# The first eight attention score rows of a hybrid encoder layer, asked for in another order

## The chip, the cores and the metric

The kernel runs on one core of one Trainium2 chip. The metric is the device time of one execution in microseconds (us). Three runs of the kernel before took 1035.21, 1035.52 and 1036.41 us; the median is 1035.52.

## What is computed

One encoder layer over 1024 tokens of width 1024, in float32. One normed input is multiplied by one projection matrix. Its columns feed two token mixers: group A, windowed attention with 8 query heads over 2 key/value heads, partial rotary turning of the first 16 of 64 dimensions and a sink logit per head; and group B, neighbourhood attention of 8 heads over a 16 x 64 grid. Both results are normed, joined and multiplied by an output matrix, and a gated MLP with a short convolution and a last norm follow. The change lies in group A:

```python
def block(args):
    ...
    s = jnp.einsum('bqgrd,bkgd->bgrqk', q_i, k_i).astype(jnp.float32) * scale
    ...
    m = jnp.maximum(jnp.max(s, axis=-1), sink_gr)
    p = jnp.exp(s - m[..., None])
    denom = jnp.sum(p, axis=-1) + jnp.exp(sink_gr - m)
    o = jnp.einsum('bgrqk,bkgd->bgrqd', p.astype(v_i.dtype), v_i)
    o = o / denom[..., None].astype(o.dtype)
```

## The kernel before, in words

All matrices stand transposed on the chip, features on the 128 partitions and tokens along the row. The projection is made in 18 jobs (`Project`, line 624), each for 128 output columns in two halves of 512 tokens. A half is eight k steps, and a k step is three matmuls (lines 172 to 174), since each operand is kept as a high and a low part. The weights of a job come by DMA (line 150), are split on ScalarE (line 156) and VectorE or GpSimd (line 157), and the product leaves PSUM through line 269 or 273 on VectorE.

Attention is cut into units. A unit of group A is one block of 128 queries of one key/value head: four score rows, one for each of its query heads 0 to 3, and then the products with the values. A score row (`q_step`, line 509) is

- two matmuls on TensorE (line 434) into one of two PSUM banks named s: 128 queries by 256 keys in block 0, which has one neighbour, by 384 in block 1;
- on VectorE mask, sum and minimum out of that bank (line 464), which frees the bank;
- the exponential with its row sum on ScalarE (line 468), the reciprocal on VectorE (line 469);
- then by `PATH_A = "DPTT"`: head 0 splits on ScalarE and VectorE (lines 483, 485) and head 1 on ScalarE and GpSimd (lines 472, 478, 479), and both are transposed by a DMA on SyncE's queue (line 490); heads 2 and 3 are scaled on GpSimd (line 472) and later transposed on TensorE (line 496), and copied out by ScalarE and VectorE (lines 499, 500).

The value products (line 523) read the transposed rows, heads 0 and 1 first, heads 2 and 3 after.

Heads 0 and 1 of the first key/value head come from projection job 1, heads 2 and 3 from job 2. After its projection a job's tile is turned by position (`rotate`, lines 285 to 291, through DMAs and VectorE) and split into two parts that are laid over each other on the partitions. For job 1 the split writes into place (`split_first`, line 305). For job 2 (`split_pair`, line 294) the second part is made by line 299 on VectorE, and DMAs (lines 300 and 302) carry the pieces to their partitions. Job 3, the key and value of the second key/value head, comes next: lines 357 to 362 and 375 measure and split its value, lines 287 to 289 turn its key, and line 341 splits that.

TensorE's order is written out by hand (`manual_schedule`): the list `queue_q` holds all score rows by unit and head, and `fill(n)` puts n k steps of the projection between them. The other engines and the DMA queues are ordered by the scheduler from the program and its priorities, so the order written for TensorE changes theirs too. Each of them works off its order from the front.

The first eight score rows, those of units 0 and 1, are asked for ahead of the unit loop (lines 960 to 964): two at once, then four k steps, then each further row behind two k steps, and two k steps at the end. Then the unit loop begins with the transposes and value products of unit 0.

## Time and profile before

| | |
|---|---|
| profiled execution | 1035.44 us |
| span of its instructions | 1033.6 us |
| TensorE (PE) busy | 1011.4 us, 98% |
| VectorE (DVE) busy | 880.5 us, 85% |
| ScalarE (ACT) busy | 677.1 us, 66% |
| GpSimd (POOL) busy | 215.1 us, 21% |
| mean granted TensorE clock | 0.996 |

Times inside the profile count from the first instruction. Matmuls are pipelined: one of 512 columns is shown as 0.39 us long, though the next one starts 0.23 us after it, so the pace of TensorE is read from the starts. A bracket such as `[3.04 <-DVE hl L485]` is the idle time just before an instruction and what the profile takes for its releaser; where several things are waited for, the one named is that whose signal came last by the profile, and it can be another.

### The profile page before, as it was taken

Reading aid. Unit: us, or ns where it says so; the run is one execution under the profiler, and the core shown is the slowest. Engines: PE = TensorE matmul, PEld = TensorE weight load, DVE = VectorE, ACT = ScalarE, POOL = GpSimd, SP = SyncE. Lnnn points to the kernel's source line nnn. Section 1 sums busy time; section 2 is a strip of 40 time slices with the busy share of each in tenths; the row PEclk is TensorE's granted clock in tenths of the full one; section 3 lists DMA queues with packets and bytes.
Section 4 is the critical chain, followed back from the end, with each engine's and each line's share of the span. In section 5 each row is a group of like instructions: output and inputs, shape, how many; then the busy total and the mean of one; then the engine's idle time right before and its main releaser. Section 6 shows DMA issues by size and latency. Waiting matters only on the chain.

```text
span 1033.6 us, 15700 instructions
## 1 busy us (share of the span) xinstructions
PE 1011.4 (98%) x5102; PEld 578.2 (56%) x5102; DVE 880.5 (85%) x1746; ACT 677.1 (66%) x1242; POOL 215.1 (21%) x340
## 2 busy tenths in 40 slices
PE   8989999999999999999999999999999999999996
PEld 6877777777775545544444444444444444444446
DVE  6798988766898699899898988888888879999864
ACT  7557787777687587645778777754535656555551
POOL 1325555676866301000000000000000000000002
PEclk9999999999999999999999999999999999999999
DMA  8566574777689775300687867733232779878734
GB/s 306 201 138 129 106 131 100 149 164 140 139 179 221 233 260 199 112 1 28 219 271 265 278 232 248 252 110 135 83 112 102 247 251 307 306 244 269 260 133 163
DMA packets 143939, 191.80 MB, mean 186 GB/s; under 512 B 77360, under 2 KB 88112, under 8 KB 143856
## 3 DMA queue, kind: packets, MB, share of 16 engines
q1 hardware_dynamic: 133264, 164.84, 55.4%
q10 hardware_dynamic: 10592, 25.95, 6.6%
q8 instruction: 40, 0.66, 0.3%
q14 instruction: 43, 0.35, 0.1%
HBM read 132.81 MB, written 28.57 MB: 156 GB/s over the span
## 4 chain that ended last, share of the span: by engine, by line
PE 73%; DVE 5%; DMA 1%; ACT 1%; issue 1%; POOL 0%; DVEq 0%; ACTq 0%; POOLq 0%
PE dn L1186 6%; PE dn L1185 6%; PE dn L1184 6%; PE pj L180 6%; PE z L1186 5%; PE z L1184 5%; PE z L1185 5%; PE y L1186 4%; PE y L1184 4%; PE y L1185 4%; PE x L1184 4%; PE x L1186 4%; PE x L1185 4%; PE pj L172 2%; PE pj L174 2%; PE pj L173 2%
## 5 line engine op out<-in xcount | busy, mean ns | idle before, releaser
L1186 PEld LDWEIGHTS <-wlo 128*128 128x128 f16 x898 | 87.9, 98 | 101.3
L1184 PEld LDWEIGHTS <-whi 128*128 128x128 f16 x898 | 88.1, 98 | 100.2
L1185 PEld LDWEIGHTS <-whi 128*128 128x128 f16 x898 | 87.9, 98 | 100.3
L1185 PE MATMUL dn<-xd,whi 128*128 128x512 f16 (+1 forms) x330 | 120.4, 365 | 0.0
L1186 PE MATMUL dn<-xd,wlo 128*128 128x512 f16 (+1 forms) x330 | 120.4, 365 | 0.0
L1184 PE MATMUL dn<-xd,whi 128*128 128x512 f16 (+1 forms) x330 | 120.4, 365 | 0.0
L172 PE MATMUL pj<-xgh,whi 128*128 128x512 f32 x248 | 107.3, 433 | 0.0
L468 ACT ACTIVATE p<-p,nm 128x385 f32<-128x385 f32 (+3 forms) x128 | 74.8, 585 | 38.9 <-DVE nm L464 32.1
L1184 PE MATMUL z<-hg,whi 128*128 128x512 f16 x264 | 100.1, 379 | 0.0
L1185 PE MATMUL z<-hg,whi 128*128 128x512 f16 x264 | 100.1, 379 | 0.0
L1186 PE MATMUL z<-hg,wlo 128*128 128x512 f16 x264 | 100.1, 379 | 0.0
L174 PE MATMUL pj<-xgh,wlo 128*128 128x512 f32 x248 | 98.5, 397 | 0.0
L173 PE MATMUL pj<-xgl,whi 128*128 128x512 f32 x248 | 97.9, 395 | 0.0
L1158 ACT ACTIVATE whi<-ws,m 128x512 f16<-128x512 f32 (+1 forms) x96 | 65.8, 708 | 37.1 <-DVE ws L1325 22.6
L1159 DVE SCALAR_TENSOR_TENSOR wlo<-ws,m,whi 128x512 f16<-128x512 f32 (+1 forms) x96 | 70.1, 740 | 16.5 <-ACT whi L1158 16.3
L1039 POOL TENSOR_TENSOR back<-back,cst 128x4 f32<-128x4 f32 (+1 forms) x7 | 2.8, 394 | 356.8 <-DVE back L1038 356.8
L1173 ACT ACTIVATE scan<-scan 128x1024 f32<-128x1024 f32 (+1 forms) x60 | 61.0, 1017 | 16.6 <-DMA scan<-in_w_down_dram 13.7
L1158 ACT ACTIVATE whi<-raw,m 128x512 f16<-128x512 f32 (+1 forms) x78 | 51.4, 699 | 15.7 <-DMA raw<-in_w_down_dram 9.0
L1159 DVE SCALAR_TENSOR_TENSOR wlo<-raw,m,whi 128x512 f16<-128x512 f32 (+1 forms) x78 | 55.4, 731 | 6.4 <-ACT whi L1158 6.2
L1184 PE MATMUL y<-hg,whi 128*128 128x512 f16 x160 | 60.6, 379 | 0.0
L1185 PE MATMUL y<-hg,whi 128*128 128x512 f16 x160 | 60.6, 379 | 0.0
L1186 PE MATMUL y<-hg,wlo 128*128 128x512 f16 x160 | 60.6, 379 | 0.0
(298 smaller groups left out, 2463.8 us busy)
## 6 DMA issues: line engine op xcount, KB each, us to landing
xd<-x SPq DMA_DIRECT2D x77, 256.0 KB, 5.4
raw<-in_w_down_dram SPq DMA_DIRECT2D x64, 256.0 KB, 3.5
x<-c ACTq DMA_DIRECT2D x22, 512.0 KB, 2.8
scan<-in_w_gate_dram SPq DMA_DIRECT2D x18, 512.0 KB, 4.0
scan<-in_w_up_dram SPq DMA_DIRECT2D x18, 512.0 KB, 4.2
raw<-in_w_gate_dram SPq DMA_DIRECT2D x18, 512.0 KB, 4.4
raw<-in_w_up_dram SPq DMA_DIRECT2D x18, 512.0 KB, 3.6
raw<-in_w_in_dram SPq DMA_DIRECT2D x32, 256.0 KB, 3.1
```

Source lines behind the costliest of these rows:

```text
L172: nc.tensor.matmul(ps, w[0], x[0][:, tsl(h)], start=first, stop=False)
L173: nc.tensor.matmul(ps, w[0], x[1][:, tsl(h)], start=False, stop=False)
L174: nc.tensor.matmul(ps, w[1], x[0][:, tsl(h)], start=False, stop=last)
L180: nc.tensor.matmul(ps, a, b, start=i == 0 and b is x[h][0] and a is w[0], stop=i == len(ws) - 1 and a is w[1])
L468: nc.scalar.activation(p[:, 0:e], p[:, 0:e], AF.Exp, bias=nm, scale=-1.0, accum_out=sm)
L1039: nc.gpsimd.tensor_tensor(back, back, unit_back.to_broadcast([128, n]), op=ALU.mult)
L1158: mark["whi"] = nc.scalar.activation(hi, src, AF.Copy, scale=by)
L1159: nc.vector.scalar_tensor_tensor(lo, src, by, hi, op0=ALU.mult, op1=ALU.subtract)
L1173: nc.scalar.activation(t, t, AF.Square, accum_out=dst)
L1184: nc.tensor.matmul(ps, w[0], x[0], start=first and i == 0, stop=False, skip_group_check=True)
L1185: nc.tensor.matmul(ps, w[0], x[1], start=False, stop=False, skip_group_check=True)
L1186: nc.tensor.matmul(ps, w[1], x[0], start=False, stop=last and i == len(ws) - 1, skip_group_check=True)
```

## The change

The first eight entries of `queue_q` are put into another order: heads 0 and 1 of unit 0, heads 0 and 1 of unit 1, heads 2 and 3 of unit 0, heads 2 and 3 of unit 1. The k steps between them become two before every row from the third on, and four after the eighth, in place of four, then two each, and two after. Rows, k steps and their sum are the same.

```diff
         queue_q = [(u, s) for u in range(len(flat)) for s in flat[u][0]]
+        queue_q[0:8] = [queue_q[4 * u + j] for j0 in (0, 2) for u in range(2) for j in (j0, j0 + 1)]
...
             if i > 1:
-                fill(4 if i == 2 else 2)
+                fill(2)
             run_q([item])
-        fill(FILL1 - 10)
+        fill(FILL1 - 8)
```

On TensorE, before, this stands behind the first two score rows and their four k steps; `q_572` and `q_573` are heads 2 and 3, `q_540` and `q_541` heads 0 and 1, and the number behind `s` or `pj` is that of the buffer:

```order
L174 MATMUL pj_646<-xgh_124,wlo_500 128x512
L434 MATMUL s_654<-ka_534,q_572 128x256
L434 MATMUL s_654<-kb_535,q_572 128x256
L172 MATMUL pj_646<-xgh_201,whi_499 128x512
L173 MATMUL pj_646<-xgl_202,whi_499 128x512
L174 MATMUL pj_646<-xgh_201,wlo_500 128x512
L172 MATMUL pj_646<-xgh_217,whi_499 128x512
L173 MATMUL pj_646<-xgl_218,whi_499 128x512
L174 MATMUL pj_646<-xgh_217,wlo_500 128x512
L434 MATMUL s_671<-ka_534,q_573 128x256
L434 MATMUL s_671<-kb_535,q_573 128x256
```

And this stands in the changed kernel from the third and fourth score row, heads 0 and 1 of unit 1, to the fifth, the first that reads `q_572`:

```order
L434 MATMUL s_669<-ka_534,q_541 128x384
L434 MATMUL s_669<-kb_535,q_541 128x384
L172 MATMUL pj_662<-xgh_201,whi_499 128x512
L173 MATMUL pj_662<-xgl_202,whi_499 128x512
L174 MATMUL pj_662<-xgh_201,wlo_500 128x512
L172 MATMUL pj_662<-xgh_217,whi_499 128x512
L173 MATMUL pj_662<-xgl_218,whi_499 128x512
L174 MATMUL pj_662<-xgh_217,wlo_500 128x512
L434 MATMUL s_690<-ka_534,q_572 128x256
L434 MATMUL s_690<-kb_535,q_572 128x256
```

The first row that needs head 2 moved from the third place to the fifth; before the change four k steps lie ahead of it, and now four k steps and two other score rows. From the first transpose of unit 0 on, TensorE's order is the same.

VectorE, before, behind the second score row's line 464 and the first reciprocal:

```order
L157 TENSOR_TENSOR wlo_584<-raw_579,whi_583 128x512
L482 TENSOR_SCALAR by_620<-sm_613 128x1
L469 RECIPROCAL sm_630<-sm_630 128x1
L287 TENSOR_TENSOR f_172<-f_172,turns_170 64x128 x2
L357 TENSOR_REDUCE top_716<-t_503 64x1
L485 SCALAR_TENSOR_TENSOR hl_619<-p_611,by_620,hl_619 128x2x128
```

And in the changed kernel at the same place, `s_646` and `s_669` being the third and fourth score row:

```order
L464 ISA p_649,nm_650<-s_646,cst_89,nsink_168 128x384
L464 ISA nm_650 128x1
L482 TENSOR_SCALAR by_620<-sm_613 128x1
L469 RECIPROCAL sm_630<-sm_630 128x1
L157 TENSOR_TENSOR wlo_584<-raw_579,whi_583 128x512
L464 ISA p_672,nm_673<-s_669,cst_89,nsink_168 128x384
L464 ISA nm_673 128x1
L485 SCALAR_TENSOR_TENSOR hl_619<-p_611,by_620,hl_619 128x2x128
```

Two more score rows are worked off here, ahead of job 3's turning and measuring (lines 287 and 357). Those and what follows from them (lines 288, 289, 358 to 362, 375, 341) come later.

VectorE, before, where the transposed rows of unit 0's head 3 are written (`pt_863`), which the third value product of unit 0 reads:

```order
L269 TENSOR_TENSOR t_767<-pj_768,rstd1_370 128x512
L469 RECIPROCAL sm_839<-sm_839 128x1
L500 TENSOR_TENSOR turned_653<-pt_863,turned_653 128x2x128
L482 TENSOR_SCALAR by_844<-sm_839 128x1
L464 ISA p_871,nm_872<-s_868,cst_89,nsink_168 128x384
```

And in the changed kernel:

```order
L469 RECIPROCAL sm_839<-sm_839 128x1
L500 TENSOR_TENSOR turned_689<-pt_863,turned_689 128x2x128
L482 TENSOR_SCALAR by_844<-sm_839 128x1
L464 ISA p_871,nm_872<-s_868,cst_89,nsink_168 128x384
L464 ISA nm_872 128x1
L287 TENSOR_TENSOR f_172<-f_172,turns_170 128x128
```

One of the two line 287 instructions of job 4's turning, and its lines 288 and 289 further on, now stand behind this `L500`; before the change they stand ahead of it. On VectorE the two orders agree again from about the 380th of its 1,748 instructions on, on SyncE's queue from about the 95th of 564.

## The prediction

> **What bounds the kernel now.** I read the page's first lines first, then the busy time by stages, then TensorE's waits, then the rows around the longest of them. The page:

> ```profile
> span 1033.6 us, 15700 instructions
> PE 1011.4 (98%) x5102; PEld 578.2 (56%) x5102; DVE 880.5 (85%) x1746; ACT 677.1 (66%) x1242; POOL 215.1 (21%) x340
> ```

> TensorE is busy 98% of the span, so the end moves only by what TensorE waits or runs slowly. The profiled execution took 1035.44 us, 1.84 more than its span and 0.08 under the median of 1035.52; sums below are made against 1035.44. A measurement of this kernel can tell about 0.2%, 2.07 us, from no change. By stages (columns: stretch, length, busy time with counts of PE, PEld, DVE, ACT, POOL, granted clock, DMA share, GB/s):

> ```profile
> 62.20:65.20 3.00, 0.04 (x1) 0.00 (x0) 2.94 (x9) 1.53 (x4) 1.48 (x3) 1.00 0.89 225
> 65.20:70.00 4.80, 4.72 (x16) 3.91 (x17) 3.92 (x15) 2.38 (x5) 1.36 (x6) 0.64 0.36 77
> 77.00:100.00 23.00, 21.79 (x126) 16.30 (x124) 20.41 (x67) 16.77 (x44) 11.99 (x24) 1.00 0.71 136
> 200.00:225.00 25.00, 25.00 (x137) 19.54 (x137) 15.51 (x58) 15.24 (x37) 17.70 (x26) 1.00 0.85 171
> 430.00:800.00 370.00, 370.00 (x1726) 169.05 (x1724) 328.25 (x487) 235.57 (x372) 7.95 (x23) 1.00 0.48 164
> ```

> TensorE stands still for 3 us from 62.2, and then runs 4.8 us at a mean clock of 0.64. VectorE is nearly full there and until 100. Later, as from 200 on, TensorE is full and VectorE has 9.5 us free in 25: what is gained or lost ahead of that is carried to the end. TensorE's waits of the whole run (total, times, longest), and the rows of its timeline at them:

> ```profile
> PE pt L496 <- POOL p L472: 3.8, 4, 1.2
> PE s L434 <- DVE hl L485: 3.0, 1, 3.0
> ...
> 59.21 0.28 PE L434 MATMUL s<-kb,q 128*128 128x256 f32 x1
> 59.33 0.40 PE L172 MATMUL pj<-xgh,whi 128*128 128x512 f32 x1
> ...
> 65.28 0.36 PE L434 MATMUL s<-ka,q 128*128 128x256 f32 x1 [3.04 <-DVE hl L485]
> 77.10 0.38 PE L496 MATMUL pt<-cst,p 128*128 128x128 f32 x2
> 81.30 0.41 PE L523 MATMUL o<-turned,v 128*128 128x256 f16 x2
> 87.83 0.55 PE L496 MATMUL pt<-cst,p 128*128 128x128 f32 x3 [1.21 <-POOL p L472]
> ```

> The longest wait is that of the third score row, head 2 of unit 0, at 65.28. The page puts it down to line 485, which writes nothing that this row reads. It reads the query tile of heads 2 and 3, and that comes by DMA; the tile's rows, and the DMAs' in SyncE's queue:

> ```profile
> L302 SPq DMA_DIRECT2D q<-t x1: 547/547/547, 61.4 to 61.4; - x1
> DMA to landing us min/median/max: 3.8/3.8/3.8
> ...
> 60.76 1.16 SPq L302 DMA_DIRECT2D q<-t x2
> ```

> The second of the two is issued at 61.4 and lands 3.8 later, at 65.2: that is the releaser.

> **The change part by part.** *The wait and the clock.* The 3.04 us go. The slow stretch behind them loses 4.80 x (1 - 0.64) = 1.73 more. No other row of stillness is followed by one: the stretch 77 to 100 holds the wait of 1.21 and has a clock of 1.00. So 1.73 is put down to the long wait, and 4.77 us are to be had.

> [...]

> *What is late next on TensorE.* The third row is now head 0 of unit 1 with 384 keys; its query tile is there, but it needs the first score bank, which line 464 of the first row frees:

> ```profile
> 59.51 1.21 DVE L299 SCALAR_TENSOR_TENSOR t<-t,q 128x1024 fp32r<-128x1024 f32 x1
> 60.65 0.48 DVE L464 CUSTOM_DVE_ANT_0 p<-s,cst,nsink 128x256 f32<-128x256 f32 x1
> ```

> The pace of TensorE's projection matmuls and of a 384 wide score's two, by their starts:

> ```profile
> 60.03 0.40 PE L172 MATMUL pj<-xgh,whi 128*128 128x512 f32 x1
> 60.26 0.39 PE L173 MATMUL pj<-xgl,whi 128*128 128x512 f32 x1
> 70.17 0.33 PE L434 MATMUL s<-ka,q 128*128 128x384 f32 x1
> 70.34 0.34 PE L434 MATMUL s<-kb,q 128*128 128x384 f32 x1
> ```

> Line 464 ends at 61.13. TensorE is there after two k steps: 59.33 + 6 x 0.23 = 60.71. It waits 0.45 and starts at about 61.2. Two score rows of 2 x 0.17 = 0.34 and two pairs of k steps of 6 x 0.23 = 1.38 bring it to 64.6, where head 2 of unit 0 needs the DMA of 65.2. The SyncE and VectorE orders up to that DMA are unchanged, so it lands as before: 0.6 more.

> So 1.05 of waits replace 4.77: TensorE reaches the first transpose, line 496, 3.72 earlier, at 73.4 instead of 77.1. The scores themselves and the k steps cost what they did.

> *VectorE behind it.* It must keep up, and this is where I expect part of the gain to go back. TensorE's third value product of unit 0 (81.30) reads the rows that line 500 writes at 80.98; TensorE comes there at 81.30 - 3.72 = 77.6. VectorE's stretch from the first line 464 to the end of that line 500, with the rows that now stand behind it and the two idle times of note:

> ```profile
> 60.65:81.38 20.73, 17.69 (x81) 14.13 (x80) 18.77 (x59) 11.92 (x29) 7.33 (x18) 0.92 0.71 150
> ...
> 67.98 1.28 DVE L375 SCALAR_TENSOR_TENSOR vhl<-t,down,vhl 64x1024 f16<-64x1024 f32 x1 [0.69 <-ACT vhl L374]
> 72.11 0.69 DVE L269 TENSOR_TENSOR t<-pj,rstd 128x512 f32<-128x512 f32 x1 [0.69 <-PE pj L174]
> 77.19 0.64 DVE L287 TENSOR_TENSOR f<-f,turns 128x128 f32<-128x128 f32 x2
> 77.87 0.43 DVE L288 TENSOR_TENSOR f<-f,turns 128x256 f32<-128x256 f32 x1
> 78.34 0.61 DVE L289 TENSOR_TENSOR f<-f 128x256 f32<-128x256 f32 x1
> 80.98 0.40 DVE L500 TENSOR_TENSOR turned<-pt,turned 128x256 f16<-128x256 f32 x1
> ```

> 18.77 of 20.73 are busy, 1.96 idle. Half of line 287 (0.32), line 288 (0.43) and line 289 (0.61) move behind: 1.36 less work, 17.41. With no idle time line 500 would end at 60.65 + 17.41 = 78.06, with all of it at 80.02. The wait for TensorE (0.69) goes, since TensorE is ahead by then; the wait for ScalarE in front of line 375 stays, since its scale still comes just before it; of the other 0.58 I keep half. That gives 78.06 + 0.69 + 0.29 = 79.04, against 81.38: TensorE waits 1.4 at this product and is 2.34 ahead. The bounds are 81.38 - 80.02 = 1.36 and TensorE's own 3.72 - 0.41, 3.3.

> *The wait at 87.83.* Its chain runs through ScalarE and GpSimd:

> ```profile
> 83.67 1.05 ACT L297 ACTIVATE q<-t 128x1024 fp32r<-128x1024 f32 x1
> 84.62 0.51 ACT L478 ACTIVATE stage<-p 128x384 f16<-128x384 f32 x1
> ...
> 85.21 1.76 POOL L479 TENSOR_TENSOR stage<-p,stage 128x384 f16<-128x384 f32 x1 [1.15 <-ACT stage L478]
> 87.19 1.57 POOL L472 TENSOR_SCALAR p<-p,sm 128x384 f32<-128x384 f32 x2
> ```

> Line 478 stood behind job 4's line 297; now line 297 comes after it, up to 1.05 less. The wait of 1.21 can shrink by as much, or not at all, if the reciprocal (line 469) on VectorE is then the last; I take 0.45, a little under the middle. Sum: 2.34 + 0.45 = 2.8.

> *What is moved past.* SyncE's transposes of unit 1 now stand ahead of job 3's DMAs and of one weight load (line 150). That load and its split on ScalarE, before:

> ```profile
> 70.64 1.00 SPq L150 DMA_DIRECT2D raw<-in_w_in_dram  x1
> ...
> 86.75 0.63 ACT L156 ACTIVATE whi<-raw 128x512 fp32r<-128x512 f32 x1
> ```

> 16 us lie between them and cover it; past that TensorE would wait for each further microsecond. Job 3's pieces are for the second key/value head, whose first unit is the ninth; the seven units between cover them. Both cost nothing.

> The other engines' orders stay shuffled for some way after 88; with 2.6 us idle on VectorE in 77 to 100 and 9.5 from 200 to 225, I give this no mean effect and 1 us to either side. Forecast: 1035.44 - 2.8 = 1032.64, say 1032.7.

> **The rivals.** *VectorE sets the pace.* It is busy 89% from 77 to 100; if none of its idle time closes up, only the moved 1.36 is gained: 1035.44 - 1.36 = 1034.1, no difference that can be told. For it: each idle time has a chain behind it. Against: 0.69 of it waits for the very TensorE that comes earlier. 0.22.

> *The change doesn't reach the wait.* If the third row had waited for VectorE's line 485, as the page names it, the fifth would wait in its place: 1035.4. The landing at 65.2 speaks against it. 0.04.

> *The clock drop is not the wait's.* Then the new order keeps it, and 3.72 - 1.73 = 1.99 remain: 1033.45, just inside what can't be told. Against: it begins right behind the wait, and the median of three runs is within 0.08 of this one. 0.06. [...]

> *Slower: the waits fall into half clock.* If VectorE closes up nothing, TensorE waits 80.02 - 77.6 = 2.4 at the third value product, not far from the 3.04 that dropped the clock; another 1.73 then makes 1.36 - 1.73 = -0.37, 1035.8. If the same happens again at the transpose of 87.83, another 1.73: 1037.5. It decides from a second drop on. Against it: 1.21 of stillness left the clock at 1.00. One drop 0.03, two 0.05.

> **How the numbers follow.** Forecast (2.1 to 4 us gained) 0.60; the rivals 0.22, 0.04, 0.06, 0.03 and 0.05. Faster by over 0.2%: 0.60. Within: 0.22 + 0.04 + 0.06 + 0.03 = 0.35. Slower: 0.05. The range: its low end is all of 3.72 with 0.45 at 87.83, 1031.3; its high end takes in the paced case and the unreached wait, 1035.4. Outside lie the slower cases and what gains more than 4.2.

> **What would show it.** Right: the third score row starts at about 61.2 with 0.45 idle before it, the fifth at 65.3 with 0.6, no clock below 1.00 from 60 to 80, the first line 496 at 73.4, the third value product waiting about 1.4 for line 500, the line 496 of before's 87.83 at about 85. Wrong: a wait of over 2 us left at 65, a second stretch under full clock, or TensorE back at before's times by 100.

## The result and the profile after

The changed kernel took 1031.77 us (median of 6 runs, 1030.7 to 1032.37), the kernel before beside it 1035.34 us (6 runs, 1033.7 to 1036.41): a ratio of 0.9964, with a 95% interval of 0.9953 to 0.9974. The profiled execution took 1031.43 us against 1035.44. Of these 4.0 us, 0.84 are not the change's: the first score row, ahead of which every engine's order is that of before, starts at 58.02 in this profile and at 58.86 in that of before. Both profiles are compared from there on, and S+18.24 means 18.24 us behind the start of the first score row.

The page's first lines:

```profile
span 1029.6 us, 15701 instructions
PE 1009.7 (98%) x5102; PEld 576.6 (56%) x5102; DVE 878.2 (85%) x1746; ACT 676.7 (66%) x1242; POOL 216.6 (21%) x340
```

The first three stretches of before, by stages (length, busy time of PE, PEld, DVE, ACT and POOL, granted clock, DMA share, GB/s):

```profile
62.20:65.20 3.00, 2.70 (x14) 2.05 (x13) 2.97 (x10) 2.94 (x8) 2.29 (x5) 1.00 0.60 189
65.20:70.00 4.80, 4.80 (x25) 4.08 (x24) 4.71 (x12) 2.27 (x7) 2.64 (x5) 1.00 0.52 102
77.00:100.00 23.00, 21.64 (x124) 16.16 (x123) 21.86 (x73) 17.71 (x47) 11.47 (x25) 1.00 0.83 153
```

TensorE, which did nothing in the first of these, now works 2.70 of 3.00 us; the second has a clock of 1.00 in place of 0.64; VectorE is fuller than before (4.71 of 4.80 in the second, in place of 3.92, and 21.86 of 23 in the third, in place of 20.41). TensorE's waits (total, times, longest) and its rows at the places that the prediction spoke of:

```profile
PE pt L496 <- POOL p L472: 1.9, 3, 1.0
PE o L523 <- DVE by L482: 1.2, 1, 1.2
```

```profile
60.31 0.44 PE L434 MATMUL s<-ka,q 128*128 128x384 f32 x1 [0.28 <-DVE nm L464]
64.32 0.36 PE L434 MATMUL s<-ka,q 128*128 128x256 f32 x1 [0.30 <-DMA q<-t]
72.44 0.38 PE L496 MATMUL pt<-cst,p 128*128 128x128 f32 x2
75.96 0.44 PE L496 MATMUL pt<-cst,p 128*128 128x128 f32 x2 [0.63 <-DVE turned L500]
79.07 0.27 PE L523 MATMUL o<-turned,v 128*128 128x256 f16 x1 [1.23 <-DVE by L482]
84.14 0.55 PE L496 MATMUL pt<-cst,p 128*128 128x128 f32 x3
```

The wait of 3.04 is gone. In its place stand two short ones at the third and the fifth score row, a new one at 75.96, and one at the third value product (79.07). The line 496 of before's 87.83 starts at 84.14 with no wait. A bracket shows what is left after the modelled end of the matmul before. By the starts (the distance from one start to the next, less the usual one) the waits are 0.44, 0.45, 0.79 and 1.39, and there is one more of 0.3 at the first matmul of the third value product (77.58). The starts are compared in what follows, except where brackets are shown. TensorE against before, from the first score row: first line 496 at S+14.42 (S+18.24 before, 3.82 earlier), second matmul of the third value product, the one that waits, at S+21.05 (S+22.58, 1.5 earlier); line 496 of before's 87.83 at S+26.12 (S+28.97, 2.85 earlier); 3.65 earlier from 360 to 805, 3.2 at the end.

What VectorE does ahead of the third value product, and the stretch from the first line 464 to the end of that line 500:

```profile
73.15 0.29 DVE L287 TENSOR_TENSOR f<-f,turns 128x128 f32<-128x128 f32 x1 [0.55 <-DMA f<-t]
74.16 1.29 DVE L375 SCALAR_TENSOR_TENSOR vhl<-t,down,vhl 64x1024 f16<-64x1024 f32 x1 [0.64 <-ACT vhl L374]
75.47 0.42 DVE L500 TENSOR_TENSOR turned<-pt,turned 128x256 f16<-128x256 f32 x1
76.35 1.21 DVE L341 TENSOR_TENSOR kb<-t,ka 64x1024 fp32r<-64x1024 f32 x1
78.62 0.40 DVE L500 TENSOR_TENSOR turned<-pt,turned 128x256 f16<-128x256 f32 x1
```

```profile
59.77:79.02 19.25, 16.74 (x81) 13.10 (x80) 17.74 (x56) 12.01 (x29) 9.45 (x18) 1.00 0.61 139
```

The line 500 at 75.47 frees the bank for which the line 496 of 75.96 waits, and it stands behind job 3's line 375. The one at 78.62 is what the second matmul of the third product waits for (the trace names the line 482 behind it; line 500 writes the rows that the product reads), and job 3's line 341 stands ahead of it.

### The profile page after: what moved, and what is told of

Read it like the earlier page. It is cut to its first block, busy times and chain, and to the rows that moved or that the text cites. A ratio compares the mean times of both kernels' runs of the same rounds, so it can differ in the third digit from the quotient of the medians.

```text
span 1029.6 us, 15701 instructions
## 1 busy us (share of the span) xinstructions
PE 1009.7 (98%) x5102; PEld 576.6 (56%) x5102; DVE 878.2 (85%) x1746; ACT 676.7 (66%) x1242; POOL 216.6 (21%) x340
## 4 chain that ended last, share of the span: by engine, by line
PE 73%; DVE 5%; DMA 1%; ACT 1%; issue 1%; POOL 0%; ACTq 0%; DVEq 0%; POOLq 0%
PE dn L1185 6%; PE dn L1186 6%; PE dn L1187 6%; PE pj L180 6%; PE z L1185 5%; PE z L1186 5%; PE z L1187 5%; PE y L1185 4%; PE y L1186 4%; PE y L1187 4%; PE x L1185 4%; PE x L1186 4%; PE x L1187 4%; PE pj L172 2%; PE pj L174 2%; PE pj L173 2%
## 5 line engine op out<-in xcount | busy, mean ns | idle before, releaser
L172 PE MATMUL pj<-xgh,whi 128*128 128x512 f32 x248 | 106.7, 430 | 0.0
L174 PE MATMUL pj<-xgh,wlo 128*128 128x512 f32 x248 | 97.9, 395 | 0.0
L173 PE MATMUL pj<-xgl,whi 128*128 128x512 f32 x248 | 97.4, 393 | 0.0
```

The source lines that it names most:

```text
L172: nc.tensor.matmul(ps, w[0], x[0][:, tsl(h)], start=first, stop=False)
L173: nc.tensor.matmul(ps, w[0], x[1][:, tsl(h)], start=False, stop=False)
L174: nc.tensor.matmul(ps, w[1], x[0][:, tsl(h)], start=False, stop=last)
```

## The experiments

Each kernel was timed beside the kernel before on the same chip. Ratios are to that, with the 95% interval.

**The order alone.** The new order with the old filling:

```diff
+        queue_q[0:8] = [queue_q[4 * u + j] for j0 in (0, 2) for u in range(2) for j in (j0, j0 + 1)]
```

> The new order of the eight score rows with the old k steps between them (four ahead of the third row, two ahead of each further one, two at the end). S is the start of the first score row; before, the first transpose (line 496) stands at S + 18.2, in the changed kernel at S + 14.4. Now the third and the fifth row should wait for nothing, and the first transpose stand at about S + 13.5. Theory (from the first transposes on VectorE sets the pace): the second matmul of unit 0's third value product still stands at about S + 21, and the time is within 0.7 us of the changed kernel's 1031.8. Rival (TensorE's own waits count in full): the 1.05 us that are still waited in the changed kernel come off the time too, 1030.7.

1036.46 us, ratio 1.0007 (0.9999 to 1.0016): no gain at all, and both expected times were missed. TensorE's rows with a wait, then two neighbouring stretches of 3.41 us, and VectorE's row with the long wait:

```profile
75.04 0.41 PE L496 MATMUL pt<-cst,p 128*128 128x128 f32 x2 [0.35 <-DVE turned L500]
76.81 0.27 PE L523 MATMUL o<-turned,v 128*128 128x256 f16 x1 [0.31 <-ACT turned L499]
78.97 0.28 PE L523 MATMUL o<-turned,v 128*128 128x256 f16 x1 [1.89 <-DVE by L482]
86.92 0.55 PE L496 MATMUL pt<-cst,p 128*128 128x128 f32 x3 [1.20 <-POOL p L472]
```

```profile
75.69:79.10 3.41, 1.21 (x7) 0.58 (x6) 3.38 (x8) 1.11 (x3) 0.57 (x1) 1.00 0.56 89
79.10:82.51 3.41, 3.41 (x12) 2.68 (x12) 1.54 (x4) 2.50 (x5) 0.49 (x2) 0.50 0.97 185
```

```profile
82.00 0.62 DVE L464 CUSTOM_DVE_ANT_0 p<-s,cst,nsink 128x384 f32<-128x384 f32 x1 [1.67 <-PE s L434]
```

Up to the first transpose everything came as the theory had it: the waits at the third and fifth rows are filled, and TensorE is 4.89 ahead of before (S+13.35). The second matmul of the third value product stands at S+20.51, for the expected 21. There it has run into VectorE's queue. The second and third of these waits leave it 1.21 us of work in 3.41, and the next 3.41 us run at a clock of 0.50. There TensorE's score comes so late that now VectorE waits for it (1.67), and the transposes at 86.92 wait 1.20 for the chain behind that score as they did before the change. Each engine has stood still for the other in turn, and of the 4.89 some 0.5 are left at 86, and nothing at the end.

**The filling alone.** The old order, two k steps ahead of the third row (in place of four) and four at the end:

> The old order of the score rows with the new k steps (two ahead of each row from the third on, four at the end). Theory (the third row waits for a DMA that lands at a fixed time): the third row comes two k steps sooner and waits about 4.4 us instead of 3.0, one stretch of half clock stays, the first transpose stands at S + 19.6, and the time is 1.4 us over the kernel before, 1036.7. Rival (the new placing of the k steps is what helps): faster than before by 2 us or more, 1033 or less.

1036.5 us, ratio 1.0013 (1.0004 to 1.0022). The third row waits 4.5 in its trace and half clock comes with it, as the theory had it (the 11 runs have a mean granted clock of 0.9948, the 27 of the kernel before beside them 0.9959); the rival is dead. Each half of the change alone gains nothing.

**The wait halved without a new order.** The old order, six k steps ahead of the third row, none at the end:

> The old order, with six k steps ahead of the third row, two ahead of each further one and none at the end: the wait for the DMA is cut from 3.0 to about 1.7 us and not removed. Theory (the half clock belongs to the length of that wait): no stretch under full clock after it, the first transpose at S + 15.1 (1.38 + 1.73 sooner than before), time 1032.2 to 1033.2. Rival (the half clock is not the wait's): the stretch stays, the first transpose stands at S + 16.9 and the time is about 1034.

1037.68 us, ratio 1.0024 (1.0015 to 1.0033), some 4.5 over the theory's time. The row waits 1.9 by the starts and no half clock follows it (the matmuls of the k steps behind it start 0.23 apart): so far the theory. But waits of 1.25 and 3.28 appear at 75.91 and 80.34 with 6.8 us of half clock from 78.79, and the time is higher than before. That the wait shrinks is no gain in itself.

**The wait filled without a new order.** Ten k steps ahead of the third row, one ahead of each further one, one at the end:

> The order of before, but ten k steps of projections ahead of the third score row in place of four, one ahead of each further row in place of two, and one at the end: the long wait filled with work instead of reordered. Theory: the wait at 65 goes to under 0.5 and no half clock follows it, so TensorE is 4.5 earlier at the first transpose; what is left at the end is set by whether the waits for VectorE that follow stay under about 2 us in 3.4: if so 1033, if they bunch, half clock comes near 78 and the time is 1036. Rival (the gain is the reordering's own): 1035.5 without any half clock from 60 to 90.

1036.78 us, ratio 1.0018 (1.0009 to 1.0027), the second branch of the theory. The long wait is gone and the first transposes come 3.6 earlier (3.82 in the changed kernel). Then two transposes wait 2.1 and 2.7, up to 77.47 and 96.59, and half clock (0.50) sets in at 76.94 and 97.42.

**The wait kept, the clock drop taken away.** The kernel before, with 22 needless matmuls in the wait:

```diff
+            for i in range(more):
+                nc.tensor.matmul(ps[:, 0:n], qa[0, 0][0][:, 0:128], ka[0][0][:, 0:n], start=True, stop=True)
...
+                    ps, _ = scores(qa[g, j // 2][j % 2], ka[g], b, more=22 if (g, b, j) == (0, 0, 2) else 0)
```

> The kernel before, every order kept, with 22 matmuls that are not needed (head 0's query block against the key, written into the third score row's own bank ahead of its two real ones) filling the wait of 3.04 us; the row still waits for its query tile's DMA. Theory: the half clock behind the wait (1.73 us) comes of TensorE standing still for most of one stretch of 3.41 us; with 2.5 us of it filled no half clock is seen from 60 to 75, the first transpose comes 1.7 earlier against the first score row (S+16.5 in place of S+18.24), and of that some 0.6 to 1.7 is left at the end: 1033.8 to 1034.9. Rival (the half clock has another cause, or VectorE would have set the time in any case): 1035.1 to 1035.5.

1035.03 us, ratio 0.9998 (0.9989 to 1.0007), between the theory's times and the rival's. Its stretches at the wait and behind it, TensorE's rows with a wait (lines stand two further on), and the query tile's DMAs:

```profile
62.00:65.00 3.00, 3.00 (x27) 2.96 (x26) 2.94 (x8) 1.44 (x4) 1.58 (x3) 1.00 0.35 97
65.00:70.00 5.00, 5.00 (x24) 3.98 (x23) 4.12 (x14) 2.68 (x5) 1.30 (x5) 1.00 0.32 66
```

```profile
77.90 0.55 PE L498 MATMUL pt<-cst,p 128*128 128x128 f32 x3 [1.32 <-POOL p L474]
86.99 0.55 PE L498 MATMUL pt<-cst,p 128*128 128x128 f32 x3 [1.21 <-POOL p L474]
```

```profile
58.78 1.15 SPq L302 DMA_DIRECT2D q<-t  x2
DMA to landing us min/median/max: 3.2/3.4/3.7
```

The clock stays at 1.00, and not in this trace alone: the mean granted clock of the 11 runs is 0.9972, that of the 20 runs of the kernel before beside them 0.9957. What the trace doesn't show is that the filling did it. VectorE and these DMAs are further ahead of TensorE in this execution than in that of before: the second DMA is issued at 59.4 (S+0.7, for S+2.5) and lands by 63.1, and TensorE reaches the row at 61.88, so without the needless matmuls it would have waited some 1.2 (an estimate from these rows) and not 3.04. That the drop goes with standing still is read from the stretches of the other kernels (last section). TensorE is 2.0 ahead at the first transpose; 1.3 of that go to a new wait of 1.32 at 77.90, 0.6 are left up to 240, and the timing shows nothing. The prediction's 1.73 was not to be had alone.

**TensorE put back, orders kept.** The changed kernel with 8 such matmuls ahead of the fifth row:

> The changed kernel, every order kept, with 8 matmuls that are not needed (0.96 us, into the row's own bank) ahead of the fifth score row: they fill its wait of 0.45 and put TensorE 0.5 further back. Theory (VectorE's queue sets the time from the first transposes on): the waits at 75.96 and 79.07 shrink by 0.5 in sum, and 0.2 or less of the 0.5 is left from S+30 on against the changed kernel's trace; the time is 1031.8. Rival (TensorE sets it): 0.5 is left at S+30 and later, 1032.3.

1032.2 us, ratio 0.9971 (0.9959 to 0.9983). In this trace the second score row itself waits 0.63 for its query, so its times are taken from that row on (58.26 in the changed kernel, 59.74 here; lines two further on):

```profile
74.56 0.38 PE L498 MATMUL pt<-cst,p 128*128 128x128 f32 x2
77.66 0.44 PE L498 MATMUL pt<-cst,p 128*128 128x128 f32 x2 [0.21 <-DVE turned L502]
80.77 0.27 PE L525 MATMUL o<-turned,v 128*128 128x256 f16 x1 [1.22 <-DVE by L484]
```

The first transpose comes 0.64 later (74.56 - 59.74 against 72.44 - 58.26), the third product 0.22 (80.77 - 59.74 against 79.07 - 58.26), and 0.24 stay up to 107. Two thirds of the 0.64 vanish in the wait at the changed kernel's 75.96, which falls from 0.63 to 0.21: there TensorE's own work doesn't set the time, VectorE's queue does, for the most part. The trace is nearer the theory (0.2 or less left) than the rival (0.5). The time (0.4 above the changed kernel's, with intervals wider than that) can't tell them apart.

**Less work on VectorE.** The changed kernel without the low part of the second key/value head's value (line 375 of job 3; zeros stand in its place):

```diff
+            if n == 64 and mark.get("begun"):
+                nc.gpsimd.memset(hl[rows, :, 1], 0.0)
+            else:
                 nc.vector.scalar_tensor_tensor(hl[rows, :, 1], src, down[rows], hl[rows, :, 0], op0=ALU.mult, op1=ALU.subtract)
```

> The changed kernel with one VectorE instruction of job 3 left out: line 375 (1.29 us, and 0.64 us idle before it) no longer computes the low part of the second key/value head's value; GpSimd writes zeros there instead, early. Theory (TensorE's two waits at 75.96 and 79.07 come from VectorE's line 500 standing behind line 375): both waits together shrink from 1.9 us to under 0.6, the second matmul of the third value product moves from S + 21.05 to S + 19.1 to 19.6, and the time falls by 0.5 to 1.9 us to 1029.9 to 1031.3, unless a later wait takes it back. Rival (they are set by ScalarE, GpSimd or the transposes themselves): both waits stay, and the time is 1031.8.

1030.86 us (5 runs), ratio 0.9956 (0.9944 to 0.9969). The wait at 75.96 is gone and TensorE is 0.8 further ahead at the end than in the changed kernel's trace. But waits of 0.61 and 1.29 remain at the two matmuls of the third value product, over the 0.6 expected, since line 341 still stands ahead of that line 500, and the second of them starts at S+20.46, where 19.1 to 19.6 was expected. The time is as expected, but its interval overlaps the changed kernel's: the timing alone doesn't show that this kernel is faster.

**The same with the order alone.** The first kernel of this part without that low part:

> The new order with the old filling, and the low part of the second key/value head's first value (line 375 of that job on VectorE, 1.2 us) left out. Theory: the order alone gained nothing because its waits for VectorE at 75.04, 76.81 and 78.97 (0.35 + 0.31 + 1.89) lay within 3.4 us and were followed by half clock; with 1.2 us of VectorE work less ahead of them their sum falls to about 1.3, no half clock follows at 79, and the time comes to 1032.5 (1.7 for the clock, 1.2 for the waits, some more at 86.92). Rival: the clock drop has nothing to do with the waits, or the placing of the k steps costs by itself: half clock stays near 79 and the time stays at 1035 or over.

1033.03 us, ratio 0.9983 (0.9974 to 0.9991). No half clock follows the waits in the trace, the 11 runs have a mean granted clock of 0.9972, for 0.9952 with the order alone, and the kernel that had gained nothing is now faster than before. 1.2 us of VectorE's work were worth some 2.5 us here (1.0007 less 0.9983, of 1035), since the clock went with them: 0.0020 of 1035 us (0.9972 less 0.9952) are 2.1 of these 2.5 (an estimate). The rival is dead, and the time is 0.5 over the theory's. But the step in between was wrong: the waits didn't fall to 1.3 in sum. They are 0.37, 1.02 and 1.05 by the brackets, 2.44 for 2.55. In this trace they fall otherwise into the stretches of the clock: one ends at 77.69, within the second wait, and the next, up to 81.10, has 1.70 us of work in place of 1.21 (what followed such stretches: last section).

**VectorE's work put off, nothing left out.** The changed kernel with job 3's stacking (lines 339 and 341) at a later place of the schedule:

> The changed kernel, with the stacking of the second key/value head's key (line 339 on ScalarE, line 341 of 1.21 us on VectorE) put off to a later place; nothing is left out. Theory: TensorE's third value product of unit 0 waits for VectorE's queue (1.23 in the changed kernel), so it waits 0.3 or less here, TensorE is about 1 us further ahead there, and the time is 1030.8 (0.5 to 1 better than the changed kernel's 1031.8). Rival: other VectorE work moves up into the place and the wait stays: 1031.8.

1037.37 us, ratio 1.0021 (1.0013 to 1.0030). The rows of VectorE and TensorE that it turns on (lines one further on from 411):

```profile
92.01 1.21 DVE L341 TENSOR_TENSOR kb<-t,ka 64x1024 fp32r<-64x1024 f32 x1
93.15 1.01 DVE L501 TENSOR_TENSOR turned<-pt,turned 128x384 f16<-128x384 f32 x2
```

```profile
93.83 0.52 PE L497 MATMUL pt<-cst,p 128*128 128x128 f32 x3 [2.61 <-DVE turned L501]
```

At the third product it does what the theory said, in part: the wait falls to 0.76, and TensorE is 0.5 further ahead than in the changed kernel at 89. Then line 341 stands in front of two copies at 93.15, and a transpose waits 2.61 for them. That costs 2.8 against the changed kernel, and another 2.5 are lost up to 147, at waits that weren't followed. At this place VectorE's queue had no room: what was put off was paid a little later, and more dearly. Other places weren't tried.

**The low part on other engines.** The changed kernel with line 375's work on ScalarE and GpSimd for job 3:

```diff
+                nc.scalar.activation(src, src, AF.Copy, scale=down[rows])
+                nc.gpsimd.tensor_tensor(hl[rows, :, 1], src, hl[rows, :, 0], op=ALU.subtract)
```

> The changed kernel, with the low part of the second key/value head's value (line 375, 1.2 us on VectorE) made by ScalarE (scaling in place, some 1 us) and GpSimd (a subtraction of 64x1024, 2 to 4 us); nothing is left out. Theory: VectorE's 1.2 us go as they did when the line was left out, the wait near 76 vanishes, and the time is 1030.9, provided GpSimd's two idle stretches after 74 (0.97 and 2.22 us) take the subtraction without making its copies of line 463 late. Rival: GpSimd's copies come late, line 464 waits for them on VectorE, and the time is 1032.5 to 1034.

1037.81 us, ratio 1.0025 (1.0014 to 1.0035), worse than the rival too. GpSimd's subtraction, and a row of VectorE that starts while it runs, next to one that VectorE waits for:

```profile
76.31 2.14 POOL L377 TENSOR_TENSOR vhl<-t,vhl 64x1024 f16<-64x1024 f32 x1 [1.05 <-PE pj L174]
```

```profile
76.61 0.42 DVE L504 TENSOR_TENSOR turned<-pt,turned 128x256 f16<-128x256 f32 x1 [1.58 <-ACT turned L503]
76.95 1.65 DVE L287 TENSOR_TENSOR f<-f,turns 128x128 f32<-128x128 f32 x1
```

Line 500 (504 here) waits 1.58 for ScalarE, whose half of the copy (line 503) now stands behind the scaling; and line 287, 0.29 in the changed kernel's row above, takes 1.65 and ends just behind the subtraction. VectorE loses both ways more than the 1.2 it is spared. The third product waits 2.5, and a transpose at 95.94, where the changed kernel's doesn't wait, 2.00 for another such line 504. What the rest of the 6 us over the changed kernel goes to wasn't followed.

**One k step more and one less.** The changed kernel with three, and with one, k steps ahead of the third row in place of two, made up for behind the eighth:

> The changed kernel with three k steps of projections in place of two ahead of the third score row, and one less at the end of the rows: half way back to the old filling. Theory (TensorE's lead is worth only what VectorE can follow): the wait of 0.44 ahead of the third row goes, TensorE is some 0.2 to 0.4 further ahead at the first transpose, and gives it back at the waits for VectorE's line 500 near 76 and 79; the time stays within 1 of the changed kernel's 1031.8, or goes up by 1.7 to 3 if these waits come to about 2 us within one stretch of 3.41 us and half clock follows. Rival (every wait taken from TensorE's queue is a gain): 1031.3 or less.

> The changed kernel with one k step of projections in place of two ahead of the third score row, and one more at the end of the rows. So far two steps gave 1031.8, three 1032.5, four 1036.5. Theory (what counts is how VectorE's queue falls, not TensorE's lead): the wait ahead of the third row grows from 0.44 to 1.1, and the waits near 76 and 79 shrink by as much; the time is within 0.7 of 1031.8, unless VectorE's own order, which this shifts too, opens a new wait of over 1 us on TensorE. Rival (fewer steps ahead of the row are better throughout): 1031.1 or less.

Three: 1032.53 us, ratio 0.9973 (0.9962 to 0.9983). The waits near 76 and 79 grow to 1.32 and 1.64 by the starts, half clock doesn't follow, the time stays within 1 of the changed kernel's: the theory. One (the third row waits 1.14, as expected): 1034.58 us, ratio 0.9986 (0.9977 to 0.9995), which neither expected in this form. Its rows on SyncE's queue and TensorE:

```profile
59.06 0.50 SPq L302 DMA_DIRECT2D q<-t  x1
60.47 0.33 SPq L150 DMA_DIRECT2D raw<-in_w_in_dram  x1
60.90 0.47 SPq L302 DMA_DIRECT2D q<-t  x1
```

```profile
65.19 0.36 PE L434 MATMUL s<-ka,q 128*128 128x256 f32 x1 [1.98 <-DVE top L357]
```

```profile
62.56:65.98 3.42, 1.44 (x8) 0.92 (x7) 3.36 (x9) 1.75 (x5) 1.81 (x5) 1.00 0.66 143
65.98:69.39 3.41, 3.41 (x11) 2.73 (x10) 3.12 (x13) 1.70 (x6) 2.51 (x4) 0.50 0.61 117
```

With the k step moved, the scheduler ordered the other engines anew, and a weight load now stands between the query tile's two DMAs. The second is issued at 60.90, S+3.72, in place of S+2.54 in the changed kernel, the fifth row waits 1.98 for it, and half clock follows (0.50 for 3.41 us): before's wait in small. Its 11 runs lie between 1031.67 and 1035.09, with granted clocks from 0.995 to 0.998, so the drop of the trace doesn't take place in all of them. So with one, two, three and four k steps ahead of the third row the new order gives 1034.6, 1031.8, 1032.5 and 1036.5: the two halves of the change belong together, and no neighbour on either side is better. No kernel that does the whole work was faster than the changed one.

## Why the prediction was right, and where its steps were off

The forecast was 1032.7 with a gain of 2.8; measured are 1031.77 and, by the medians, 3.6. Point by point:

*The releaser and the new waits.* Right. The fifth row is released by the DMA in name now; the waits are 0.44 and 0.45 for 0.45 and 0.6, and the first transpose comes 3.82 earlier for 3.72.

*The half clock.* Right: it is gone with the wait (a clock of 1.00 from 65.2 to 70, for 0.64), and filling the wait alone also took it away there (the matmuls of the k step behind the row start 0.23 apart). "4.77 to be had" was wrong as a price: the wait halved, the wait filled and the clock drop taken away gained nothing each. What TensorE saved was worth only what VectorE let through: of the 4.89 us with the order alone some 0.5 were left at 86.

*VectorE at the third product.* The mechanism was right and its size too small. Line 500 was to end 18.39 us behind the start of the first line 464 and ended 19.25 behind it. Its work is 17.74 for 17.41, and its idle time 1.51 for 0.98: line 287 waits 0.55 for a DMA, which wasn't in the sum. The work is more because lines 287 and 288 of job 3 take 0.74 and 0.67 in place of 0.26 and 0.41, beside subtractions on GpSimd (last section). Nor was the bank at 75.96 in the sum: TensorE gave 0.79 back there, 0.3 at the first matmul of the product and 1.39 (for 1.4) at the second, and is 1.5 ahead behind it in place of 2.34.

*The wait at 87.83.* 0.45 was too little; all of the 1.21 is gone. Line 478 of ScalarE, with the line 297 that stood ahead of it, GpSimd's line 479 behind it, and a row of VectorE before the change:

```profile
81.72 0.52 ACT L478 ACTIVATE stage<-p 128x384 f16<-128x384 f32 x1 [0.33 <-POOL p L472]
89.08 1.05 ACT L297 ACTIVATE q<-t 128x1024 fp32r<-128x1024 f32 x1
```

```profile
82.33 0.95 POOL L479 TENSOR_TENSOR stage<-p,stage 128x384 f16<-128x384 f32 x1 [0.64 <-ACT stage L478]
```

```profile
84.97 1.22 DVE L299 SCALAR_TENSOR_TENSOR t<-t,q 128x1024 fp32r<-128x1024 f32 x1
```

Line 297 is out of the way, as the prediction had it. Besides, line 479 takes 0.95 for 1.76, which wasn't in the sum: before, it started at 85.21, beside VectorE's line 299, and that line now stands at 90.29. The two misses, 0.84 too much at the product and 0.9 too little here, cancel: 2.85 ahead at this place for the 2.8 of the sum. That the sum came out nearer than its terms is luck.

*The later shuffle.* Within its bounds of 1: TensorE is 3.67 ahead at before's 111, for the most part because the wait of 1.2 at 110.95 is gone too, less 0.8 at a new one at 104.98. A wait of 0.6 at 114.56 takes that back (3.07), and smaller ones bring it to 3.65 by 147, 0.8 more than at 87.83.

*A premise that the prediction didn't state.* It took the order for the cause and the placing of the k steps for a detail. The order alone gains nothing. And the rival in which waits fall into half clock, at 0.08, was worth more as a mechanism than that: half clock (0.50) followed waits in four of the experiments, the order alone, the halved and the filled wait and the one step less. In the changed kernel it lay near. Its trace has half clock only at the end, from 1024.73; counted back in steps of 3.4133 from there (last section), the stretch that holds the wait of 79.07 begins at 75.83:

```profile
75.83:79.24 3.41, 1.93 (x10) 1.30 (x11) 3.41 (x10) 1.21 (x5) 1.15 (x1) 1.00 0.76 121
```

TensorE is idle 1.48 in it. That rival knew of a wait of 1.21 that left the clock alone and one of 3.04 that dropped it, and counted with one wait of 2.4; in the stretches of the last section that lie inside the kernels, 1.92 us of idle time and more (3.41 - 1.49) were followed by half clock and 1.90 and less (3.41 - 1.51) weren't, in one wait or in several.

What stays open: a k step can't be moved here without the scheduler ordering VectorE and SyncE anew, so how much of the distance between the kernels with two, three and four steps is the step's own wasn't separated.

## What to carry to other kernels

A wait taken from TensorE, busy 98% of the span, was worth only what the engines that feed it could follow with (the wait filled alone: 3.6 us earlier at the first transposes, nothing at the end), so price a wait by the neighbour's queue over the next 20 us, and look for the next wait behind each one that goes, PSUM banks included. Where a scheduler orders the other engines, as here, a shifted filler step is a change of all queues (one k step less: 1034.6 us for 1031.8), and its neighbours on both sides belong in the measurement. Short waits close together can be followed by what a long one is: with the order alone 0.31 and 1.89 us, in one stretch of 3.41, were followed by 3.41 us at a clock of 0.50, as the 3.04 before the change were.

## What the hardware showed beside this

```profile
94.01:97.42 3.41, 0.83 (x6) 0.77 (x7) 3.31 (x13) 2.82 (x8) 1.72 (x3) 1.00 0.94 172
97.42:100.83 3.41, 3.41 (x11) 2.35 (x9) 2.19 (x7) 1.48 (x4) 0.19 (x2) 0.50 0.81 189
```

```profile
76.33:79.74 3.41, 1.62 (x9) 1.13 (x9) 3.41 (x8) 1.04 (x3) 0.61 (x1) 1.00 0.68 134
79.74:83.15 3.41, 3.41 (x20) 2.72 (x20) 3.41 (x13) 2.66 (x8) 0.94 (x3) 1.00 0.53 102
```

```profile
336.65:340.06 3.41, 1.51 (x11) 0.94 (x10) 1.46 (x7) 2.31 (x6) 0.85 (x3) 1.00 1.14 174
340.06:343.47 3.41, 3.41 (x21) 2.11 (x21) 1.79 (x6) 2.55 (x6) 3.05 (x5) 1.00 0.31 60
```

```profile
1024.60:1028.01 3.41, 2.26 (x20) 1.98 (x18) 0.91 (x3) 0.68 (x2) 0.00 (x0) 1.00 0.53 177
1028.01:1031.42 3.41, 1.08 (x4) 0.71 (x4) 2.47 (x7) 0.38 (x1) 1.40 (x2) 0.50 0.24 79
```

Inside the kernels, from full clock, stretches with 0.79 (before), 0.83 and 1.49 (wait filled), 1.21 (order alone), 1.31 (wait halved) and 1.44 us (one step less) of work in 3.41 were followed by half clock, those with 1.51 (low part on other engines), 1.62 (three k steps), 1.70 (order alone, less work on VectorE) and 1.93 (changed kernel) weren't. At the kernels' ends stretches with 1.12 (before, 1025.22 to 1028.63) and 0.91 (changed kernel, 1021.32 to 1024.73) were followed by half clock; but so was the one with 2.26 above, where the count fails. Why it fails there, no run shows. In the kernel with the wait halved a stretch at half clock with 1.86 of work (78.79 to 82.20) was followed by another at 0.50. The 2.61 us of waiting in the kernel with the stacking put off, ending at 93.83, left the clock at 1.00. A stretch ends at 92.76 there, counted back from the drop at the kernel's end, so that some 1.5 of the wait lie in one, which has 1.87 of work, and 1.1 in the next, which has 2.34.

*One kernel, several clocks.* The stretches lie differently from trace to trace: counted in steps of 3.4133 from a drop, one ends 0.2 us behind the first score row in the trace of the order alone, 0.4 in that of before, 0.7 in that of the changed kernel and 2.0 with one step less. And a trace shows one execution. One drop of 3.41 us to half clock is 0.0017 of the mean clock (an estimate: 3.41 x 0.5 of 1030 us). The 90 runs of the kernel before beside the experiments have mean granted clocks from 0.994 to 0.998, and the time goes with them up to 0.997: a median of 1037.06 us in the 9 runs at 0.994, of 1035.11 in the 41 at 0.996, of 1034.71 in the 19 at 0.997, of 1034.98 in the 4 at 0.998. Their mean is 0.9959, that of the changed kernel's 6 runs 0.9970.

*VectorE's and GpSimd's work side by side.* Line 287 on VectorE took 1.65 us beside GpSimd's subtraction of 64x1024, 0.29 in the changed kernel (rows above), and ended 0.15 behind it. In the changed kernel it took 0.74 at 63.70, on 64x128, beside a subtraction on GpSimd that ended at 64.30, and 0.27 right after. GpSimd's subtraction of 128x384 (line 479) took 0.92 to 0.95 in most places of the two main traces, 1.76 in before's where VectorE's line 299 had started 0.24 ahead of it, and 1.48 and 1.13 at two places of the changed kernel's (66.99 and 112.36). Whether one engine's work held up the other's, no experiment separated.
